# Four embedding squares, one low part and the f = 7 roundings put in other places of their engines' order

## The chip, the cores and the metric

The kernel runs on one core of one Trainium2 chip. The time is device time in microseconds (us); the median of three runs before the change is 703.91 us (702.66 to 705.85). The core has five engines that work side by side: TensorE (PE in the profile) multiplies matrices, VectorE (DVE) and ScalarE (ACT) work elementwise, GpSimd (POOL) does small elementwise work and issues some of the transfers, and SyncE (SP) issues the rest. Each engine takes its instructions in the order of its own queue, so an instruction that has to wait also holds up what stands behind it on the same engine.

## The reference: what is computed

One layer of a decoder block on 512 tokens of width 1024, all in float32:

```python
h = rms_norm(x, g_mix_pre);  z = h @ w_in                 # two token mixers and gates
merged = gate_pool * y_pool + gate_rnn * y_rnn
x = x + rms_norm(merged @ w_o, g_mix_post)
h = rms_norm(x, g_ffn_pre);  up = h @ w_up                # 1024 x 6144
hid = gelu(causal_dwconv(up[:, :3072])) * up[:, 3072:]
x = x + rms_norm(hid @ w_down, g_ffn_post)
ple = rms_norm(p @ w_ple_proj, g_ple_post)                # the embedding
x = x + sigmoid(rms_norm(x, g_ple_gate) @ w_ple_gate) * ple
```

The change touches the passage from the first half to the feed-forward part: the normalised `h` of the second norm (called h2 in the kernel), the statistics of the embedding's norm, and the first pairs of the product with `w_up`.

## The kernel before

**Two parts of each operand.** Products have to be nearly as exact as float32, so each operand is split into a high part (the value rounded to a shorter format) and a low part (the value less its high part). The helper `split` does that in two instructions: ACT copies into the high part (line 195, "rounding" in this document), DVE subtracts (line 191 by way of `sub`). A product is then three matmuls: high by high, high by low, low by high (lines 222 to 224).

**Seven products for eight.** The large products are done in blocks of two by two by a scheme with seven products in place of eight. The seven are called by form numbers f = 1 to 7; forms need sums and differences of blocks, of the activations (made on the chip: `form`, `form_split`) and of the weights. A pair is two column tiles of `w_up` gate and up side; there are twelve, p = 0 to 11. Pair 0 is done plainly (`up_plain`, forms 11, 21, 12, 22), since its products can begin with half of the tokens; pairs 1 to 11 are done in seven products (`up_product`). The order of forms within pair 1 is 1, 6, 2, 5, 7, 4, and from pair 2 on 1, 3 (of the pair before), 6, 2, 7, 5, 4. Weight sums of pairs 1 and 2 are made by transfers in DRAM and loaded, those of later pairs are added by DVE (line 385).

**What follows a product in the up stage.** Forms 1, 6 and 7 accumulate in the same two PSUM banks (`zb`). ACT copies the state out in between: line 1155 after form 1, 1160 after form 6, and after form 7 lines 1162 (into the gate bank `gb`) and 1163 (into the up bank `ub`). Form 4 then accumulates on top of what line 1162 has put into `gb`. The convolution and the gelu of a finished column tile start at line 1168.

**The four h2 tiles.** The normalised tokens come in four tiles of 128. `h2_tile(t)` transposes one by PE (line 1029), in two halves of one PSUM bank each. Each half gives a high part on ACT, a low part on DVE (both to the tiles named C) and two plain copies on ACT (line 1056, to tiles named m), which later make the forms. Tiles are counted 0 to 3 here; the third token tile is tile 2.

**The embedding.** `ple_tile(t)` multiplies a token tile of p with its weight, and copies the two halves out (lines 858 and 859) and to DRAM (line 861). `ple_norm(t)` then takes two squares with row sums on ACT (line 513), adds them on DVE (line 524), takes the reciprocal root on POOL (line 508) and copies the result on DVE into a small tile `rp` (line 867), which is read at the kernel's end.

**Order.** The order on PE is the order of the program. PE goes through tile 2's transposes, pair 0's forms 12 and 22 on the first half of the tokens, tile 3's transposes, form 1 of pair 1 and then pair 0 on the second half:

```python
O_AFTER = (("up", 11), ("up", 21), ("tr", 2), ("up", 12), ("up", 22), ("tr", 3), ("p1", 1))
```

For the other engines a planner puts the instructions in an order at build time, by priority (the order of the program, raised by `tc.high_priority`) and by when it reckons that their inputs are there. `behind(a, b)` adds an edge: a comes after b on the engine, without a wait of its own. Names such as `last_copy`, `last_low`, `h2_done` and `z_done` remember the instructions that such edges point to; `z_done` is the last line 1163 that was traced.

**Weights.** Weights go through a ring of six raw buffers, loaded by SP (line 379 for the up stage), and rings of six high and six low parts. `weight` prepares a key four keys ahead of its use; for the up stage this leads to `up_form(p, f)`. For pair 1's forms 5 and 7 it makes the high part alone (line 416), and `later_low` makes the low part at a place that the main program names. A raw buffer is free for the next load when the low part has been made.

Of the kernel before, what the change touches and what calls it, by code (L numbers as in the profile page):

```python
# [83 lines left out]
def block_kernel(  # L84
# [21 lines left out]
    ACT, V, PE = nc.scalar, nc.vector, nc.tensor  # L106
# [13 lines left out]
    def urgent():  # L120
        return tc.high_priority(offset=URGENT)
# [3 lines left out]
    def nm(s):  # L125
        uid[0] += 1
        return f"{s}{uid[0]}"

    def bank():
        return psum.tile([P, S], F32, tag="ps", name=nm("ps"))  # L130
# [4 lines left out]
    def slot(dt=F32):  # L135
        return mid.tile([P, S], dt, tag="m", name=nm("m"))
# [10 lines left out]
    def parts_of(n):  # L147

        return [wpool.tile([P, D], F32R, tag=t, name=nm(t))[:, :n] for t in ("hi", "lo")]

    def tiny(n=1, dt=F32):
        return small.tile([P, n], dt, tag="s", name=nm("s"))

    def behind(ins, name):
        tc.add_manual_dep(
            ins.ins,
            name,
            mybir.DependencyInfo(mybir.DependencyClass.NoSync, mybir.DependencyReason.DATA),
            reason="order on the engine",
        )  # L160
# [27 lines left out]
    last_copy, last_low, last_sub, h2_done, z_done, paced = [None], [None], [None], [None], [None], [None]  # L188

    def sub(o, a, b):  # L190
        return V.tensor_tensor(o, a, b, ALU.subtract)  # L191

    def split(hi, lo, src):

        last_copy[0] = ACT.copy(hi, src)  # L195
        last_sub[0] = sub(lo, src, hi.bitcast(F32))
        last_low[0] = last_sub[0].ins.name
# [16 lines left out]
    def apart(v):  # L214
        return v.rearrange("p k (b a) -> p k a b", a=2)

    def kept(v):
        return v.rearrange("p k (a b) -> p k a b", a=2)
# [157 lines left out]
    def block(p, f):  # L376

        t = wpool.tile([P, 2, S], F32, tag="raw", name=nm("raw"), bufs=6)
        nc.sync.dma_start(t, usum[p, f] if (p, f) in usum else up_block(p, f))
        return t  # L380
# [3 lines left out]
    def add(o, a, b):  # L384
        V.tensor_tensor(o, a, b, ALU.add)

    def up_form(p, f):

        b = blocks
        if p == 0:  # L390
            t = block(0, f)
        elif p in UP_SUMS:
            t = block(p, {1: 11, 2: 21, 3: 22}.get(f, f))
        elif f == 1:
            for k in (11, 12, 22, 21):
                b[p, k] = block(p, k)
            b[p, 0] = wpool.tile([P, 2, S], F32, tag="sum", name=nm("sum"), bufs=1)
            t = b[p, 11]
        elif f == 6:
            add(b[p, 0], b[p, 11], b[p, 12])  # L400
            t = b[p, 11]
            add(t, b[p, 0], b[p, 22])
        elif f == 7:
            t = b[p, 12]
            add(t, t, b[p, 22])
        elif f == 4:
            t = b[p, 21]
            add(t, b[p, 11], t)
        else:
            t = b[p, {2: 21, 3: 22, 5: 0}[f]]  # L410
        if p == 0 and f != PLAIN[0]:
            late.append((f, t))
            return
        hi, lo = (v.rearrange("p (j c) -> p j c", j=2) for v in parts_of(D))
        if (p, f) in ((1, 5), (1, 7)):
            ins = ACT.copy(hi, t)
            behind(ins, h2_done[0])
            later[f] = hi, lo, t
            ready["up", p, f] = (hi, lo)
            return  # L420
        split(hi, lo, t)
        if p == 1 and f != 1:
            behind(last_copy[0], h2_done[0])
        if (p, f) == (1, 4):
            behind(last_sub[0], hid_done[0])
        if p > 2 and f == 6:
            behind(last_copy[0], z_done[0])
        if p > 1 and f == 3:
            behind(last_copy[0], z6_done[p])
        ready["up", p, f] = (hi, lo)  # L430

    def later_low(f):
        hi, lo, t = later[f]
        last_sub[0] = sub(lo, t, hi.bitcast(F32))
        last_low[0] = last_sub[0].ins.name
# [11 lines left out]
    def prep(key):  # L447
        if key[0] == "up" and key not in parts:
            up_form(*key[1:])
            return  # L450
# [40 lines left out]
    def weight(key, ahead=AHEAD):  # L491
        i = order.index(key)
        while nxt[0] <= min(i + ahead, len(order) - 1):
            prep(order[nxt[0]])
            nxt[0] += 1
        return ready[key]
# [1 line left out]
    def pick(t, a, b):  # L498
        return t[0][:, a:b], t[1][:, a:b]

    last_pow, last_square, last_stat = [None], [None], [None]

    rb = const.tile([P, S], F32, tag="rb", name="rb")

# [6 lines left out]
    def square(v, in_order=True, after=None):  # L511
        s = tiny()
        ins = ACT.activation(rb, v, AF.Square, scale=1.0 / 32.0, accum_out=s)  # L513
        if after is not None:
            behind(ins, after)
        if in_order:
            if last_square[0] is not None:
                behind(ins, last_square[0])
            last_square[0] = ins.ins.name
        return s  # L520

    def rstd_from(sums):
        v = tiny()
        last_stat[0] = V.scalar_tensor_tensor(v, sums[0], EPS, sums[1], ALU.add, ALU.add).ins.name  # L524
        return rsqrt(v)

    def rstd_of(halves, in_order=True, after=None):
        return rstd_from([square(v, in_order, after) for v in halves])
# [40 lines left out]
    for a in range(2):  # L569
        xt = xtok[a]  # L570
        for b in range(2):
            v = xt[:, 2 * b : 2 * b + 2, :]
            t = 2 * a + b
# [7 lines left out]
    for k in range(KD):  # L581
        w = weight(("rx", k // 2), ahead=3)
# [27 lines left out]
    mabs, e, f, s, s2, ncol, n2col = sp  # L610
# [234 lines left out]
    h2f_done, z_copied, hid_done, summed = [None], [None], [None], {}  # L845
# [17 lines left out]

    def ple_norm(t, outs, after):
        s = rstd_of(outs, in_order=False, after=after)
        rp[t] = const.tile([P, 1], F32, tag=f"rp{t}", name=f"rp{t}")
        V.tensor_copy(rp[t], s)

# [70 lines left out]
    for m in range(KD):  # L939
        w = weight(("wpo", m))  # L940
# [85 lines left out]
    def transposed(a):  # L1026
        ps = bank()
        for q in range(4):
            PE.transpose(ps[:, q * P : (q + 1) * P], a[:, q * P : (q + 1) * P], ident)  # L1029
        return ps  # L1030
# [9 lines left out]
            nc.sync.dma_start(xr[t, h], x[t * P : (t + 1) * P, h * S : (h + 1) * S])  # L1040
    h2n, h2f = {}, {}

    def h2_tile(t):
        for h in range(2):
            ps = transposed(h2n[t, h]).rearrange("p (k c) -> p k c", k=4)
            hi, lo = (v[h][t // 2][:, :, t % 2 * P : (t % 2 + 1) * P] for v in (h2h, h2l))
            with tc.high_priority(offset=2 * URGENT if t else URGENT):
                split(kept(hi), kept(lo), apart(ps))
                h2_done[0] = last_copy[0].ins.name
            b, c = divmod(t, 2)  # L1050
            q = 10 * b + h + 11
            if c == 0:
                h2f[q] = {k: slot() for k in (0, 2)}
            for k in (0, 2):
                v = kept(h2f[q][k].rearrange("p (k c) -> p k c", k=2)[:, :, c * P : (c + 1) * P])
                h2f_done[0] = ACT.copy(v, apart(ps[:, k : k + 2, :])).ins.name

# [20 lines left out]
    def x2_sum(t, pair):  # L1080
        with urgent():
            add_norm(pair, g_post, [xr[t, 0], xr[t, 1]])

    def x2_out(t, after=None, stat=None):
        res = [xr[t, 0], xr[t, 1]]
        for h in range(2):
            nc.sync.dma_start(x2d[t * P : (t + 1) * P, h * S : (h + 1) * S], res[h])
        with urgent():
            r = rstd_of(res, after=after)
            for h in range(2):  # L1090
                h2n[t, h] = slot()
                ins = V.scalar_tensor_tensor(h2n[t, h], res[h], r, g_pre[h], ALU.mult, ALU.mult)  # L1092
                if stat is not None:
                    behind(ins, stat)
# [94 lines left out]
    ple_outs = []  # L1189
    for t in range(NT):  # L1190
        with tc.high_priority(offset=3 * URGENT):
            outs = ple_tile(t)
        ple_outs.append(outs)
        if t == 1:
            h2_tile(1)
            late_splits()
            x2_sum(3, (oz[1], o5[:, 1]))
            x2_out(2, h2_done[0], last_stat[0])
        if t == 2:
            x2_out(3, ple_done[0])  # L1200
    for kind, n in O_AFTER:
        if kind == "tr":
            h2_tile(n)
            for t in (n - 2) * 2, (n - 2) * 2 + 1:
                ple_norm(t, ple_outs[t], h2f_done[0])
        elif kind == "up":
            up_plain(n, 0)
        else:
            up_product(n, 1)
# [221 lines left out]
    for h in range(2):  # L1431
        for t in range(NT):
            i = 2 * (t % 2) + h
            o = temp()
            v = ple[t // 2][:, i, :]
            ins = V.scalar_tensor_tensor(v, v, rp[t], gp[:, h, :], ALU.mult, ALU.mult)
# [3 lines left out]
            for a, b in parts:  # L1440
                ps = bank()
                for k in range(KD):
                    if (h, t, k) == (0, 1, 3):
                        x3_tile(2)
                    w = weight(("wpg", k // 2, h), ahead=AHEAD if h or t > 1 else 3 - k // 2)
# [86 lines left out]
```

## Time and profile before

| | |
|---|---|
| median of three runs | 703.91 us |
| the profiled execution: its time | 703.09 us |
| the profiled execution: span from first to last instruction | 701.3 us |
| PE busy | 692.9 us, 99% of the span, 4423 matmuls |
| DVE busy | 591.7 us, 84% |
| ACT busy | 454.4 us, 65% |
| POOL busy | 97.1 us, 14% |
| granted TensorE clock | 1.000 |
| chain that ended last | PE 89%, DVE 4%, DMA 3%, ACT 2% |

The profile is of one execution. In a timeline each row has the start in us from the span's first instruction, the duration, the engine, the line, the operation, the tile written and the tile read, and in brackets the time for which the engine was idle before, with the instruction that ended it. Neighbouring instructions of one kind stand in one row with a count (x4). A list of waits has the engine and line that waited, what it waited for, and three numbers: total us, times, longest. A row of the table by stretch has the stretch, its length, the busy time and the number of instructions of PE, the weight loads, DVE, ACT and POOL, then the granted clock, the transfers' share and GB/s. Matmuls overlap: the next one starts before the last has ended, so PE can be busy all the time and still lose a little.

### The profile page before, as it was taken

What the parts mean: (1) busy time and instruction counts of PE and PEld (TensorE: products, weight loads), DVE (VectorE), ACT (ScalarE), POOL (GpSimd) and SP (SyncE); (2) the same over time, 40 slices, a digit from 0 to 9 for tenths busy, and PEclk for the clock granted to TensorE, in tenths of its full rate; (3) what the DMA queues carried; (4) which work ended last, traced back from release to release, by engine and by line L of the source; (5) the groups of instructions that cost most, each with busy time, mean ns of one, the idle gap of its engine ahead of it and who ended that gap; (6) DMA issues with size and microseconds to landing.
All of it is one profiled execution on the core that took longest, in us unless ns stands there. A gap on an engine that the chain in (4) does not pass through costs nothing.

```text
span 701.3 us, 11599 instructions
## 1 busy us (share of the span) xinstructions
PE 692.9 (99%) x4423; PEld 637.9 (91%) x4423; DVE 591.7 (84%) x772; ACT 454.4 (65%) x693; POOL 97.1 (14%) x123
## 2 busy tenths in 40 slices
PE   8999999999999999999999999999999999999997
PEld 7888888888889998899999999999999888888886
DVE  5698735999849998897999999999999988989962
ACT  5857789934538575487966667766667747665631
POOL 0311231412000000112011211111210210001100
PEclk9999999999999999999999999999999999999999
DMA  8999899999797897865386886896699799968111
GB/s 309 411 306 277 249 249 257 244 275 277 241 347 270 316 368 261 314 226 168 118 320 216 195 267 209 208 265 242 160 218 385 237 300 327 338 215 273 43 61 61
DMA packets 67287, 175.71 MB, mean 251 GB/s; under 512 B 6048, under 2 KB 6688, under 8 KB 66848
## 3 DMA queue, kind: packets, MB, share of 16 engines
q1 hardware_dynamic: 49808, 124.64, 49.3%
q0 software_dynamic: 17280, 50.34, 30.5%
q8 instruction: 35, 0.57, 0.3%
q14 instruction: 20, 0.16, 0.1%
q10 hardware_dynamic: 144, 0.00, 0.0%
HBM read 162.37 MB, written 62.91 MB: 321 GB/s over the span
## 4 chain that ended last, share of the span: by engine, by line
PE 89%; DVE 4%; DMA 3%; ACT 2%; issue 1%; POOL 1%; SPq 0%; DVEq 0%; ACTq 0%
PE ps L222 28%; PE ps L224 28%; PE ps L223 28%; PE ps L587 3%; DVE lo L191 1%; DMA lo<-parts 1%; PE ps L696 1%; ACT rb L513 1%; DMA x2d<-m 1%; DVE m L1092 1%; DMA raw<-in_w_rx_dram 1%; POOL s L508 1%; PE ps L1029 0%; DMA raw<-up2sum 0%; DVE C L191 0%
## 5 line engine op out<-in xcount | busy, mean ns | idle before, releaser
L191 DVE TENSOR_TENSOR lo<-raw,hi 128x1024 fp32r<-128x1024 f32 (+2 forms) x199 | 230.2, 1182 | 46.3 <-ACT hi L477 30.4
L222 PE MATMUL ps<-A,hi 128*128 128x256 f32 (+1 forms) x672 | 211.9, 315 | 0.0
L224 PE MATMUL ps<-A,lo 128*128 128x256 f32 (+1 forms) x672 | 211.5, 315 | 0.0
L223 PE MATMUL ps<-A,hi 128*128 128x256 f32 (+1 forms) x672 | 211.4, 315 | 0.0
L477 ACT CAST hi<-raw 128x1024 fp32r<-128x1024 f32 (+1 forms) x118 | 118.3, 1013 | 60.0 <-PE ps L224 20.0
L222 PEld LDWEIGHTS ps<-A,hi 128*128 128x128 f32 x672 | 128.2, 191 | 8.1 <-issue 1.0
L224 PEld LDWEIGHTS ps<-A,lo 128*128 128x128 f32 x672 | 128.3, 191 | 7.1 <-DVE lo L191 0.2
L223 PEld LDWEIGHTS ps<-A,hi 128*128 128x128 f32 x672 | 128.3, 191 | 6.7
L222 PE MATMUL ps<-C,hi 128*128 128x256 f32 x376 | 103.7, 276 | 1.3 <-ACT ps L1162 0.7
L223 PE MATMUL ps<-C,hi 128*128 128x256 f32 x376 | 103.3, 275 | 0.8 <-DVE C L191 0.8
L224 PE MATMUL ps<-C,lo 128*128 128x256 f32 x376 | 103.2, 274 | 0.0
L195 ACT CAST hi<-raw 128x1024 fp32r<-128x1024 f32 x76 | 78.8, 1054 | 21.2 <-PE ps L223 13.1
L222 PE MATMUL ps<-hi,A 128*128 128x512 f32 x224 | 85.2, 380 | 0.0
L223 PE MATMUL ps<-lo,A 128*128 128x512 f32 x224 | 84.9, 379 | 0.0
L224 PE MATMUL ps<-hi,A 128*128 128x512 f32 x224 | 84.9, 379 | 0.0
L222 PEld LDWEIGHTS ps<-C,hi 128*128 128x128 f32 x376 | 71.8, 191 | 1.9 <-ACT ps L1162 0.9
L223 PEld LDWEIGHTS ps<-C,hi 128*128 128x128 f32 x376 | 71.8, 191 | 1.1 <-DVE C L191 0.9
L224 PEld LDWEIGHTS ps<-C,lo 128*128 128x128 f32 x376 | 71.8, 191 | 0.0
L508 POOL TENSOR_TENSOR s<-s,mhalf 128x1 f32<-128x1 f32 (+1 forms) x21 | 17.4, 828 | 269.0 <-DVE s L524 247.1
L307 POOL DMA_DIRECT2D wdsum<-in_w_down_dram x36 | 33.1, 1056 | 141.5 <-ACT t L1158 62.8
L222 PEld LDWEIGHTS ps<-hi,A 128*128 128x128 f32 x224 | 42.3, 189 | 6.2 <-ACT hi L477 0.3
L224 PEld LDWEIGHTS ps<-hi,A 128*128 128x128 f32 x224 | 42.3, 189 | 6.0
(206 smaller groups left out, 1069.8 us busy)
## 6 DMA issues: line engine op xcount, KB each, us to landing
raw<-in_w_up_dram SPq DMA_DIRECT2D x46, 512.0 KB, 5.9
wdsum<-in_w_down_dram POOLq DMA_DIRECT2D x36, 512.0 KB, 7.5
raw<-in_w_in_dram SPq DMA_DIRECT2D x32, 512.0 KB, 8.4
raw<-wdsum SPq DMA_DIRECT2D x24, 512.0 KB, 8.0
raw<-in_w_down_dram SPq DMA_DIRECT2D x18, 512.0 KB, 6.5
wosum<-in_w_o_dram POOLq DMA_DIRECT2D x12, 512.0 KB, 8.6
wdsum<-wdsum POOLq DMA_DIRECT2D x12, 512.0 KB, 6.0
raw<-wosum SPq DMA_DIRECT2D x8, 512.0 KB, 5.9
```

The costliest lines, as they stand in the source:

```text
L191: return V.tensor_tensor(o, a, b, ALU.subtract)
L195: last_copy[0] = ACT.copy(hi, src)
L222: PE.matmul(o, ah, bh, start=start, stop=False, **kw)
L223: PE.matmul(o, ah, bl, start=False, stop=False, **kw)
L224: PE.matmul(o, al, bh, start=False, stop=stop, **kw)
L307: ins = nc.gpsimd.dma_start(o, i, **kw)
L477: ins = ACT.copy(hi, raw)
L508: last_pow[0] = nc.gpsimd.tensor_tensor(y, v, mhalf[:, :n], ALU.pow).ins.name
L513: ins = ACT.activation(rb, v, AF.Square, scale=1.0 / 32.0, accum_out=s)
L587: PE.matmul(rx[m], a[:, o : o + P], turns(b), start=k == 0 and i == 0, stop=k == KD - 1 and i == 2)
L696: PE.matmul(ps, bd[pr, a, o], turns(b[pr]), start=i == 0, stop=i == 2)
L1092: ins = V.scalar_tensor_tensor(h2n[t, h], res[h], r, g_pre[h], ALU.mult, ALU.mult)
```

## The change

1. In `h2_tile` for tile 2 alone, the four plain copies (line 1056) are no longer traced between the halves but at the end. Ahead of them `ple_norm` is called for embedding tiles 0 and 1. Their four squares stand behind tile 2's last high part, and the four copies behind the last square. Before, the squares stood behind the copies. For tile 3 and embedding tiles 2 and 3 the order stays as it was.
2. The weight of form 1 of pair 1 gets its high part where it did, but its low part is made by `later_low`, behind tile 2's last low part on DVE. Before, it was part of `split`.
3. From pair 2 on the rounding of form 7's weight stands behind `z_done`, the last line 1163 of the pair before. Form 6's had that edge from pair 3 on.

No operation is added or taken away.

```diff
-        if (p, f) in ((1, 5), (1, 7)):
+        if (p, f) in ((1, 1), (1, 5), (1, 7)):
             ins = ACT.copy(hi, t)
-            behind(ins, h2_done[0])
+            if f != 1:
+                behind(ins, h2_done[0])
             later[f] = hi, lo, t
...
         if p > 1 and f == 3:
             behind(last_copy[0], z6_done[p])
+        if p > 1 and f == 7:
+            behind(last_copy[0], z_done[0])
...
     def ple_norm(t, outs, after):
         s = rstd_of(outs, in_order=False, after=after)
+        ple_square[0] = last_any[0]
...
-    def h2_tile(t):
+    def h2_tile(t, then=None):
+        copies = []
...
-                h2f_done[0] = ACT.copy(v, apart(ps[:, k : k + 2, :])).ins.name
+                copies.append((v, apart(ps[:, k : k + 2, :])))
+        after = then() if then else None
+        for v, w in copies:
+            ins = ACT.copy(v, w)
+            if after is not None:
+                behind(ins, after)
+            h2f_done[0] = ins.ins.name
...
+    def early_norms():
+        after = last_copy[0].ins.name
+        for t in (0, 1):
+            ple_norm(t, ple_outs[t], after)
+        return ple_square[0]
+
     for kind, n in O_AFTER:
         if kind == "tr":
-            h2_tile(n)
-            for t in (n - 2) * 2, (n - 2) * 2 + 1:
-                ple_norm(t, ple_outs[t], h2f_done[0])
+            if n == 2:
+                h2_tile(n, early_norms)
+                low = last_low[0]
+                later_low(1)
+                behind(last_sub[0], low)
+            else:
+                h2_tile(n)
+                for t in (2, 3):
+                    ple_norm(t, ple_outs[t], h2f_done[0])
```

`last_any` and `ple_square` remember the name of the last square traced.

More of the change, by code (lines that the diff above doesn't have):

```diff
@@ L499, in pick @@
         return t[0][:, a:b], t[1][:, a:b]
-    last_pow, last_square, last_stat = [None], [None], [None]
+    last_pow, last_square, last_any, last_stat, ple_square = [None], [None], [None], [None], [None]
     rb = const.tile([P, S], F32, tag="rb", name="rb")
@@ L513, in square @@
         ins = ACT.activation(rb, v, AF.Square, scale=1.0 / 32.0, accum_out=s)
+        last_any[0] = ins.ins.name
         if after is not None:
```

## The prediction

> **What bounds the kernel now.** I read TensorE's own waits first, then the busy time by stretch, then TensorE's timeline at each wait, and last the timelines of ScalarE (ACT) and VectorE (DVE) around these places.
>
> ```profile
> PE ps L241 <- DVE mhalf L235: 1.1, 1, 1.1
> PE ps L587 <- ACT hi L474: 0.8, 1, 0.8
> PE ps L223 <- DVE C L191: 0.8, 1, 0.8
> PE ps L222 <- ACT ps L1162: 0.7, 1, 0.7
> PE ps L222 <- ACT C L195: 0.6, 1, 0.6
> ```
> ```profile
> 322.00:352.00 30.00, 27.98 (x244) 27.23 (x243) 26.11 (x42) 28.56 (x56) 4.28 (x4) 1.00 0.32 108
> 360.00:520.00 160.00, 160.00 (x1435) 160.00 (x1435) 150.34 (x163) 107.02 (x173) 27.28 (x33) 1.00 0.80 227
> ```
>
> The first fence is the whole list of TensorE's (PE) idle times. Two are the start. The other three lie close together, and the second shows where: from 322 to 352 PE is busy 27.98 of 30 us, while from 360 to 520 it is never idle, 1435 matmuls in 160 us, 0.11 us each. So PE bounds the kernel, and only what ends these few waits can shorten it. ACT (28.56) and DVE (26.11) are nearly full in that same stretch, so its work comes late by their order, not by PE's.
>
> PE around each wait (start, duration, line, then idle before and releaser):
>
> ```profile
> 324.69 0.28 PE L224 MATMUL ps<-C,lo 128*128 128x256 f32 x1
> 325.53 0.38 PE L222 MATMUL ps<-C,hi 128*128 128x256 f32 x1 [0.57 <-ACT C L195]
> 326.66 0.38 PE L223 MATMUL ps<-C,hi 128*128 128x256 f32 x1 [0.75 <-DVE C L191]
> 326.88 0.27 PE L224 MATMUL ps<-C,lo 128*128 128x256 f32 x1
> ...
> 345.52 0.28 PE L223 MATMUL ps<-A,hi 128*128 128x256 f32 x1
> 345.78 0.38 PE L224 MATMUL ps<-A,lo 128*128 128x256 f32 x1
> ...
> 349.57 0.27 PE L224 MATMUL ps<-C,lo 128*128 128x256 f32 x1
> 350.54 0.38 PE L222 MATMUL ps<-C,hi 128*128 128x256 f32 x1 [0.70 <-ACT ps L1162]
> ```
>
> A matmul's end overlaps the next, so I count starts, less the 0.11 of one. First hold: 0.73 (325.53 after 324.69) and 1.02 (326.66 after 325.53), plus 0.11 for the slow restart (326.88 after 326.66), 1.86 in all. Second: 345.78 after 345.52, 0.15, with a restart taken as the same 0.11: 0.26. It is too short to stand in the waits. Third: 350.54 after 349.57, 0.86, and a restart: 0.97. All that can be won is 1.86 + 0.26 + 0.97 = 3.09 us, 0.44% of the time.
>
> **Squares ahead of the third tile's copies.** ACT:
>
> ```profile
> 315.65 1.10 ACT L195 CAST C<-ps 128x512 fp32r<-128x512 f32 x2
> 320.82 1.24 ACT L1056 COPY m<-ps 128x256 f32<-128x256 f32 x4 [4.06 <-DVE C L191]
> 321.95 0.64 ACT L513 ACTIVATE rb<-m 128x512 f32<-128x512 f32 x1
> ...
> 324.91 1.06 ACT L195 CAST C<-ps 128x512 fp32r<-128x512 f32 x2
> ```
>
> Tile 2's two high parts end at 316.75. The next instruction, the first of four copies (L1056), waits 4.06 us for DVE's low parts of the same PSUM tile. Behind it stand four squares for embedding tiles 0 and 1 (321.95 until 324.91: 2.96 us), and only then tile 3's high parts, for which PE waits at 325.53. Embedding tiles 0 and 1 are in SBUF by then (the embedding copy at 319.50 below is tile 3's), so in front of the copies the squares fit into the idle 4.06 us: 316.7 to 319.6. Their cost there is nothing, and what covers it is that idle time; without it they would cost their 2.96 us again, before the same high parts.
>
> DVE in the same stretch:
>
> ```profile
> 313.96 3.48 DVE L191 TENSOR_TENSOR lo<-raw,hi 128x1024 fp32r<-128x1024 f32 x3
> ...
> 318.17 1.41 DVE L1092 SCALAR_TENSOR_TENSOR m<-m,s,m 128x512 f32<-128x512 f32 x2 [0.66 <-POOL s L508]
> 319.50 0.68 DVE L858 COPY m<-ps 128x512 f32<-128x512 f32 x1
> 320.11 1.28 DVE L191 TENSOR_TENSOR C<-ps,C 128x512 fp32r<-128x512 f32 x2
> 323.47 0.16 DVE L524 SCALAR_TENSOR_TENSOR s<-s,s 128x1 f32<-128x1 f32 x1 [2.09 <-ACT rb L513]
> 324.28 0.15 DVE L867 COPY rp<-s 128x1 f32<-128x1 f32 x1 [0.65 <-POOL s L508]
> ...
> 325.85 0.15 DVE L867 COPY rp<-s 128x1 f32<-128x1 f32 x1 [0.66 <-POOL s L508]
> 325.93 1.28 DVE L191 TENSOR_TENSOR C<-ps,C 128x512 fp32r<-128x512 f32 x2
> ```
>
> The three low parts (3.48, so 1.14 each from start to start) are those of the weights (0,12), (0,22) and (1,1). The last moves behind tile 2's low parts (320.11). What is between, statistic, h2 of tile 3 and an embedding copy, comes forward by 1.14, and tile 2's low parts run from 318.97 to 320.2. The copies then go at about 319.7 and 320.3 and are done near 321.0 instead of 322.06. Were the low parts no earlier, the copies would still end at 322.06 and nothing below would change by more than 0.3 us.
>
> PE, the due times:
>
> ```profile
> 321.25 1.04 PE L1029 MATMUL ps<-ident,m 128*128 128x128 f32 x8
> ...
> 322.34 0.28 PE L224 MATMUL ps<-C,lo 128*128 128x256 f32 x1
> ```
>
> Tile 3's transposes are issued from 321.25 on, and pair 1's first product follows. PE is not late here, so these times stand. Tile 3's first high part can start when the first four of the eight transposes are through, about 321.75, against 324.91: ACT is 3.16 us earlier. Its low part follows on DVE near 322.4, or 323.0 if the two statistics and copies of rp stand in front; before it was 325.93. PE wants them at 324.8 and 324.9. The first hold goes: 1.86 us.
>
> The moved low part is due at PE's third matmul of pair 1, 322.34. Behind tile 2's low parts it runs from 320.2 to 321.35: 1.0 us of slack. Its two neighbours, statistic and rp copies with a root on POOL between, are no longer at 323.47 to 325.9 but somewhere from 319 on; four small instructions of 0.15 us, whose waits cost nothing as long as the low part stands among or before them. ACT's copies also set the banks free that pair 1's first product writes, behind the transposes; ending near 321.0 they are a microsecond ahead of it.
>
> SP's queue is moved too, for the raw buffer that the low part reads is refilled later:
>
> ```profile
> 317.47 0.38 SPq L379 DMA_DIRECT2D raw<-in_w_up_dram  x1
> 320.21 0.80 SPq L861 DMA_DIRECT2D pled<-m  x2
> ```
>
> The load at 317.47, for pair 2's first weight, becomes possible at about 321.4, 3.9 us later; PE reaches that weight only after 350.54, so this is free. If SP's order keeps it ahead of the two embedding stores (320.21), these issue about 1.2 us later. Their buffers are wanted again by the forms on DVE around 325.6; a landing after that takes from DVE's lead, not from PE. I take nothing, with 0 to 1.2 us of lead as the bounds.
>
> **The second hold** is the low part of (1,7), at 344.51 on DVE, the end of a chain through ACT and DVE that starts at tile 3's high parts. The chain moves by 3.16 us and PE by 1.86, a lead of 1.3 us over a lateness of 0.26: the hold goes, 0.26 us. If the stores take 1.2 of the lead, most of it stays.
>
> **Roundings behind copies.** The chain that ended last, around the third hold:
>
> ```profile
> 344.51 1.23 DVE lo L191
> ...
> 345.80 3.27 DMA raw<-up2sum
> ...
> 349.17 1.05 ACT hi L195
> 350.22 0.28 ACT ps L1162
> ```
>
> The low part of (1,7) frees a raw buffer; the load into it (345.80) takes 3.27 us; it is pair 2's block for f = 7, since that pair's sums are loaded in the order 6, 7, 5, 4. Its rounding waits for the load at the head of ACT's queue, and the copy L1162 behind it is what PE waits for at 350.54. With the new edge the rounding stands behind L1163, so the copy goes when PE's product ends. The next product's first twelve matmuls ran until 349.57, so that end was near 348.4; with a copy near 348.7 PE has no hold at 350.54, and 0.97 us goes. The load itself comes some 3 us earlier by the chain above, so even without the edge most of this would. The rounded weight is used four products later, and the delayed rounding costs nothing.
>
> In the later pairs the first of nine alike:
>
> ```profile
> 366.10 0.38 ACT L1163 ACTIVATE ps<-ps 128x256 f32<-128x256 f32 x1
> 366.37 3.08 ACT L195 CAST hi<-raw 128x1024 fp32r<-128x1024 f32 x3
> ```
>
> Here the roundings of f = 6, 2 and 7 already stand behind L1163. The edge changes nothing there.
>
> **Sum.** 1.86 + 0.26 + 0.97 = 3.09, less 0 for the new places: 703.09 - 3.1 = 700.0 us for the profiled execution. The median shown is 703.91, 0.8 above it, so 700.8 is the forecast for a median. Bounds for what replaces a hold: 0 from the rows above, 0.8 to 1.4 from the rival below.
>
> **Where POOL could spoil it.** The roots (L508) on POOL, two of them, and what DVE ran beside the slow one:
>
> ```profile
> 317.60 0.54 POOL L508 TENSOR_TENSOR s<-s,mhalf 128x1 f32<-128x1 f32 x1 [5.60 <-DVE s L524]
> ...
> 330.89 2.66 POOL L508 TENSOR_TENSOR s<-s,mhalf 128x1 f32<-128x1 f32 x1 [5.07 <-DVE s L524]
> ```
> ```profile
> 330.73 1.21 DVE L191 TENSOR_TENSOR lo<-raw,hi 128x1024 fp32r<-128x1024 f32 x1
> ```
>
> The same 128x1 instruction took 0.54 us with DVE waiting and 2.66 us while DVE ran a low part (both inputs in SBUF) and two more such subtractions. With the change two roots come into a stretch where DVE has such work ready. The Trainium skill (SBUF — State Buffer, "Who interferes with whom") says that a VectorE instruction with two SBUF inputs contends with a GpSimd instruction that reads SBUF, and that whoever issues first has the port for the whole instruction; the 2.66 beside 0.54 agrees. By that rule the sum is 3.09 still if only the moved low part runs beside a root, as rp has no reader before the last stage, and it speaks against the change where a DVE copy of rp is queued ahead of what PE needs.
>
> **Rivals.** (1) The low part of (1,1) ends up behind both rp copies. Statistic, root and copy, twice, took 2.46 us (323.47 to 325.93); with the squares long done it is twice 0.81 (323.47 to 324.28), 1.7 with what lies between. The low part would then run from 321.9 at best, 322.6 at worst, until 323.1 or 323.8, and PE would hold at 322.34 for 0.8 to 1.4 us. For: the rp copies come earlier in the program now. Against: the low part is ready when the copies still wait for POOL, so an order by readiness puts it first. Time: 700.8 + 1.1 = 701.9. With one slow root ahead of it (2.66 for 0.54) the hold is 2.1 longer and the time 704.0; that is 0.03 of this rival's chance.
>
> (2) DVE and ACT do not keep the lead. Both are nearly full until 352; if a store or another order costs them 1.3 us or more, the holds at 345.78 and 350.54 stay in part and only the first goes: 703.91 - 1.86 = 702.0. That the change does nothing at all I count here: the squares' edge cannot be without effect, as 4.06 us of idle stand in front of them.
>
> (3) Slower. The order on ACT and DVE is worked out anew over the whole program. If in the nine pairs from 360 on the new edge draws other roundings with it, such that one of them waits at the head of ACT's queue before an L1162, each pair pays what the third hold cost, up to 0.97 us: 703.91 - 3.1 + 8.7 = 709.5. It is slower than before from 0.34 us a pair on. Against it: the roundings of f = 7 already stand where the edge wants them, and four products of 2.7 us (24 matmuls by 0.11) lie between them and their own.
>
> **Chances.** Forecast 0.62, rival 1 0.13, rival 2 0.12, rival 3 0.13. The forecast's own range is 699.5 to 701.7: 3.09 against a median that moves by a microsecond (three runs from 702.66 to 705.85). The overall range, 699.4 to 703.6, takes in rivals 1 and 2. A difference of 0.5% (3.5 us) is about what can be told from none; the holds add up to less, so faster by more needs the median's help: 0.16. Slower by over 0.5% is rival 3: 0.13. Within: 0.71.
>
> **What would show it.** Right: no PE idle between 322 and 352; four squares directly after tile 2's two high parts, with the copies at about 319.7 to 321; tile 3's first high part near 321.8; the copies L1162 of pair 1 with no rounding between them; the later pairs as before. Wrong: a wait of PE on DVE "lo" at 322.3 (rival 1), waits left at about 344 and 348 (rival 2), or idle PE after 360 (rival 3).

## The result, and the profile after

Six runs of the changed kernel had a median of 699.66 us (699.5 to 700.86); six of the kernel before, the three of the time before the change among them, 703.28 us (702.33 to 705.85). The ratio is 0.9944, with a 95% interval from 0.9923 to 0.9966: faster by 0.56%, by at least 0.34 and at most 0.77. A second comparison with more runs, below, gave 0.9960 (0.9944 to 0.9975). The profiled execution took 699.78 us, 3.31 less than the one before.

TensorE's (PE) waits after the change, the whole list, then the busy time by stretch (the columns as before), then the page's shares of the chain that ended last:

```profile
PE ps L241 <- DVE mhalf L235: 1.1, 1, 1.1
```
```profile
322.00:352.00 30.00, 30.00 (x270) 29.95 (x268) 28.76 (x44) 27.82 (x50) 3.77 (x4) 1.00 0.47 149
360.00:520.00 160.00, 160.00 (x1435) 160.00 (x1435) 150.40 (x162) 107.56 (x173) 27.90 (x34) 1.00 0.81 222
```
```profile
PE 99%; DVE 0%; ACT 0%; issue 0%
```

All three waits of the up stage are gone; the one that is left lies in the kernel's first microseconds. PE is busy for the whole of 322 to 352, with 270 matmuls where there were 244, and the rest of the up stage is as it was (1435 matmuls in 160 us). The chain that ended last, 89% on PE before, is now 99% on PE.

The places of the change, first ScalarE (ACT), then VectorE (DVE), then PE (start, duration, line, operation, idle time before). Line numbers have moved: the squares are L516, the plain copies L1065, the transposes L1034.

```profile
315.60 1.10 ACT L195 CAST C<-ps 128x512 fp32r<-128x512 f32 x2
316.56 0.68 ACT L516 ACTIVATE rb<-m 128x512 f32<-128x512 f32 x1
...
319.64 1.24 ACT L1065 COPY m<-ps 128x256 f32<-128x256 f32 x4
321.84 1.08 ACT L195 CAST C<-ps 128x512 fp32r<-128x512 f32 x2 [0.95 <-PE ps L1034]
```
```profile
318.93 1.27 DVE L191 TENSOR_TENSOR C<-ps,C 128x512 fp32r<-128x512 f32 x2
320.12 1.21 DVE L191 TENSOR_TENSOR lo<-raw,hi 128x1024 fp32r<-128x1024 f32 x1
...
323.01 1.28 DVE L191 TENSOR_TENSOR C<-ps,C 128x512 fp32r<-128x512 f32 x2
```
```profile
321.20 1.04 PE L1034 MATMUL ps<-ident,m 128*128 128x128 f32 x8
...
322.30 0.28 PE L224 MATMUL ps<-C,lo 128*128 128x256 f32 x1
...
324.75 0.28 PE L222 MATMUL ps<-C,hi 128*128 128x256 f32 x1
324.87 0.27 PE L223 MATMUL ps<-C,hi 128*128 128x256 f32 x1
...
343.63 0.28 PE L223 MATMUL ps<-A,hi 128*128 128x256 f32 x1
343.74 0.28 PE L224 MATMUL ps<-A,lo 128*128 128x256 f32 x1
```

The squares start at 316.56, directly behind tile 2's high parts, and fill the time until the copies can go at 319.64. Tile 3's high parts start at 321.84, as soon as the transposes of 321.20 let them, and before it was 324.91. Tile 2's low parts are at 318.93, the moved low part directly behind at 320.12 until 321.3, a microsecond before PE's third matmul of pair 1 (322.30). Where PE had stood for 1.86 us, it goes from 324.75 to 324.87 in step. The second hold, too short for the list of waits, is gone as well: its two matmuls (345.52 and 345.78 before) are at 343.63 and 343.74, one pitch of 0.11 apart.

The third place, ACT around the copies after form 7 of pair 1 (now L1174 and L1175):

```profile
346.39 0.36 ACT L1174 COPY ps<-ps 128x256 f32<-128x256 f32 x1 [0.69 <-PE ps L224]
...
346.94 1.07 ACT L195 CAST hi<-raw 128x1024 fp32r<-128x1024 f32 x1
```

The copy now waits for PE alone, and the rounding of pair 2 stands behind it.

### The profile page after: what moved, and what is told of

It reads as the page before. It is cut to its first block, busy times and chain, and to the rows that moved or that the text cites. A ratio compares the mean times of both kernels' runs of the same rounds, so it can differ in the third digit from the quotient of the medians.

```text
span 698.0 us, 11598 instructions
## 1 busy us (share of the span) xinstructions
PE 692.4 (99%) x4423; PEld 638.1 (91%) x4423; DVE 591.4 (85%) x772; ACT 453.9 (65%) x693; POOL 97.1 (14%) x123
## 4 chain that ended last, share of the span: by engine, by line
PE 99%; DVE 0%; ACT 0%; issue 0%
PE ps L222 31%; PE ps L223 31%; PE ps L224 31%; PE ps L591 3%; PE ps L1034 1%; PE ps L700 1%; PE ps L241 1%; PE ps L642 0%; ACT t L166 0%; DVE t L1474 0%; DVE t L1475 0%; PE ps L1160 0%; DVE m L233 0%; DVE mhalf L235 0%
## 5 line engine op out<-in xcount | busy, mean ns | idle before, releaser
L224 PEld LDWEIGHTS ps<-hi,A 128*128 128x128 f32 x224 | 42.3, 189 | 6.0
L223 PEld LDWEIGHTS ps<-lo,A 128*128 128x128 f32 x224 | 42.4, 189 | 5.9
```

The source lines that it names most:

```text
L223: PE.matmul(o, ah, bl, start=False, stop=False, **kw)
L224: PE.matmul(o, al, bh, start=False, stop=stop, **kw)
```

## The experiments

All kernels below compute the same as the kernel before. Since one difference of 1 us is 0.14%, the times alone tell little; the traces tell more. Two rows of each are enough. One is the start of tile 3's transposes, which in all traces comes before the first hold. The other is the span. What lies between them is the up stage and all that follows. For the kernel before it is 701.3 - 321.25 = 380.05 us, for the kernel after 698.0 - 321.20 = 376.8.

| kernel | tile 3's transposes | span | from there on | median us (runs) | ratio to before, 95% |
|---|---|---|---|---|---|
| before, profiled first | 321.25 | 701.3 | 380.05 | | |
| before again | 320.68 | 700.5 | 379.8 | 702.80 (12) | 0.9996 (0.9987 to 1.0006) |
| part 1: squares | 321.43 | 698.5 | 377.1 | 700.32 (11) | 0.9962 (0.9950 to 0.9974) |
| part 2: low part | 321.48 | 700.2 | 378.7 | 701.74 (12) | 0.9975 (0.9964 to 0.9985) |
| part 3: rounding | 320.68 | 699.6 | 378.9 | 701.82 (12) | 0.9981 (0.9971 to 0.9991) |
| parts 1 and 2 | 322.08 | 699.3 | 377.2 | 700.03 (6) | 0.9952 (0.9935 to 0.9970) |
| parts 1 and 3 | 321.30 | 698.1 | 376.8 | 699.94 (5) | 0.9950 (0.9930 to 0.9970) |
| parts 2 and 3 | 321.48 | 699.3 | 377.8 | 700.91 (6) | 0.9971 (0.9959 to 0.9982) |
| whole change, profiled first | 321.20 | 698.0 | 376.8 | 699.66 (6) | 0.9944 (0.9923 to 0.9966) |
| whole change again | 321.51 | 698.3 | 376.8 | 700.38 (12) | 0.9960 (0.9944 to 0.9975) |
| low part last | 321.48 | 699.2 | 377.7 | 701.08 (12) | 0.9970 (0.9958 to 0.9983) |
| root beside low part | 321.91 | 698.7 | 376.8 | 700.31 (10) | 0.9965 (0.9950 to 0.9979) |
| mixer edge | 321.26 | 698.0 | 376.7 | 700.70 (7) | 0.9963 (0.9949 to 0.9977) |

The experiments were run in three sets, each on another chip and beside its own runs of the kernel before. Only the first set (before again and parts 1, 2 and 3) has a trace of the kernel before; its 379.8 stands for all.

**The kernel before, again.** No edit.

> The kernel before, unchanged, against itself. Theory A (the 0.56% is the holds of PE, 3.1 us, and what was measured beyond it is the spread of the executions of before, 702.33 to 705.85): ratio 1.000 with an interval that is as wide as 0.002 to each side, some executions near 702.4 and some near 705, and a trace with the same three holds of 1.86, 0.26 and 0.97 us. Rival B (the slower executions have longer holds, since the third one depends on a transfer): where the profiled execution is slower than 703.1, its holds add up to more than 3.1 us.

Its waits (PE's list):

```profile
PE ps L241 <- DVE mhalf L235: 1.1, 1, 1.1
PE ps L223 <- DVE C L191: 0.8, 1, 0.8
PE ps L222 <- ACT ps L1162: 0.7, 1, 0.7
PE ps L222 <- ACT C L195: 0.5, 1, 0.5
```

The ratio of the same kernel to itself is 0.9996, and 34 runs taken beside it have a median of 703.03 us, between 701.99 and 706.24. The three holds are there again and as long (0.8, 0.7 and 0.5 in the list), so theory A holds. Rival B is about slower executions, and this one, at 702.27 us, is not slower than 703.1; it is not tested here. But the span is 0.8 us shorter, and 0.57 of it was there before the holds: the transposes are at 320.68 and not at 321.25. The wait for the first high part of the input (L587 on L474, 0.8 us in the first profile) is missing from this list. So the profiled executions of one kernel differ in the first microseconds. What PE waits for there is not the same from trace to trace; the list of parts 1 and 2 shows the largest:

```profile
PE ps L589 <- ACT A L559: 1.6, 1, 1.6
...
```

1.6 us of wait at the start (L589, the first product), and the transposes at 322.08. In the table the column behind the transposes has no such spread: the three traces without a hold in the up stage (whole change, whole change again, parts 1 and 3) agree within 0.05.

**Squares alone.** The text of the change, without the new case for form 1 of pair 1, `later_low(1)` and the edge for form 7:

```diff
             if n == 2:
                 h2_tile(n, early_norms)
-                low = last_low[0]
-                later_low(1)
-                behind(last_sub[0], low)
```

> Squares ahead of tile 2's copies alone. Theory A: the first hold goes (1.86), the second goes (0.26), since tile 3's high parts start near 322.1 where they started at 324.9, and the third shrinks from 0.97 to about 0.3, since the load of pair 2's block comes some 2.8 us earlier: about 2.8 us less than before. Rival C (the three parts are each worth their own hold): only the first hold goes, 1.9 us less, and 0.97 is left at L1162.

SP's issue of the load for pair 2's form 7, ACT behind it, and PE:

```profile
343.11 2.06 SPq L379 DMA_DIRECT2D raw<-up2sum  x2
```
```profile
346.51 1.05 ACT L195 CAST hi<-raw 128x1024 fp32r<-128x1024 f32 x1 [0.58 <-PE ps L223]
347.46 0.37 ACT L1171 COPY ps<-ps 128x256 f32<-128x256 f32 x1
```
```profile
347.65 0.27 PE L224 MATMUL ps<-C,lo 128*128 128x256 f32 x1
347.89 0.38 PE L222 MATMUL ps<-C,hi 128*128 128x256 f32 x1
```

379.8 - 377.1 = 2.7 us, and 2.7 in the medians (703.03 - 700.32). The first and the second hold are gone, and the third has shrunk without its edge, since the load goes out at 343.11 and not at 345.80: 347.89 after 347.65 is 0.13 beyond the 0.11 of one matmul, with the slow restart 0.24 in all. Theory A had 0.3; rival C's 0.97 is out. One part takes nearly everything.

**Low part alone.**

```diff
-        if (p, f) in ((1, 5), (1, 7)):
+        if (p, f) in ((1, 1), (1, 5), (1, 7)):
...
             h2_tile(n)
+            if n == 2:
+                low = last_low[0]
+                later_low(1)
+                behind(last_sub[0], low)
```

> The low part of pair 1's first weight behind tile 2's low parts, alone. Theory A: copies and squares come 1.14 us earlier, tile 3's high parts start near 323.8 where they started at 324.9, and the first hold shrinks from 1.86 to 0.6 to 0.8; the rest as before: 1.0 to 1.3 us less. Rival C (this part only makes room and is worth nothing alone): no difference, the first hold stays at 1.86.

```profile
325.03 0.28 PE L222 MATMUL ps<-C,hi 128*128 128x256 f32 x1
325.72 0.38 PE L223 MATMUL ps<-C,hi 128*128 128x256 f32 x1 [0.42 <-DVE C L191]
```

PE (above) holds for 325.72 - 325.03 - 0.11 = 0.58 and a restart of 0.1, where it was 1.86; the wait for the high part is gone, the one for DVE's low part is left. 379.8 - 378.7 = 1.1 us, 1.3 in the medians. So this part is worth something alone: it brings the copies and with them the squares forward, to 319.87 and 321.00 from 320.82 and 321.95.

**Rounding alone.**

```diff
             behind(last_copy[0], z6_done[p])
+        if p > 1 and f == 7:
+            behind(last_copy[0], z_done[0])
```

> The edge for the roundings of form 7 alone. Theory A: only pair 2's rounding changes its place, the third hold (0.97) goes, the other two stay: 1.0 us less. Rival D (the later pairs matter, too): more than 1.5 us less, or PE loses time after 360.

PE's waits, then ACT:

```profile
PE ps L241 <- DVE mhalf L235: 1.1, 1, 1.1
PE ps L223 <- DVE C L191: 0.8, 1, 0.8
PE ps L222 <- ACT C L195: 0.5, 1, 0.5
```
```profile
347.95 0.36 ACT L1164 COPY ps<-ps 128x256 f32<-128x256 f32 x1
...
348.52 1.05 ACT L195 CAST hi<-raw 128x1024 fp32r<-128x1024 f32 x1
```

The wait on ACT's copy is gone, the other two are there, and 379.8 - 378.9 = 0.9 us (1.2 in the medians). The order of instructions on all engines differs from that before in this one place: the rounding of pair 2 changes places with two copies. In pairs 3 to 11 nothing moved, as the prediction had read from the rows at 366; nothing of rival D is seen.

**Pairs of parts.** Without the edge (parts 1 and 2):

```diff
-        if p > 1 and f == 7:
-            behind(last_copy[0], z_done[0])
```

> Without the edge for the roundings. Theory A: pair 2's rounding stands ahead of L1162 again, but its load now comes near 346.1, so the copy is late by 0 to 0.2 us only: 2.9 to 3.1 us less than before, the same as the whole change within what can be told. Rival C (each part its own hold): 2.1 us less, and 0.97 at L1162.

Without the move of the low part (parts 1 and 3), the edit of the squares alone with the edge kept:

> Without the move of the low part. Theory A: the squares alone free ACT for tile 3's high parts, so the first hold stays away, and the edge takes the rest of the third: 3.1 us less, the same as the whole change. Rival C (the move has a share of its own): 1 us less gain than the whole change, as it had alone.

Without the squares (parts 2 and 3), both edits shown above in one kernel:

> Low part and edge without the squares. Theory A: as the low part alone did, the first hold shrinks to 0.6 to 0.7, the second stays at 0.25, the third goes with the edge: 2.1 us less than before. Rival C (each part its own hold): 1.0 us less, from the edge.

ACT and PE of parts 1 and 2, and of PE's waits of parts 2 and 3 the one in the up stage:

```profile
347.36 1.08 ACT L195 CAST hi<-raw 128x1024 fp32r<-128x1024 f32 x1 [0.78 <-DMA raw<-up2sum]
```
```profile
348.30 0.27 PE L224 MATMUL ps<-C,lo 128*128 128x256 f32 x1
348.76 0.38 PE L222 MATMUL ps<-C,hi 128*128 128x256 f32 x1 [0.19 <-ACT ps L1172]
```
```profile
PE ps L223 <- DVE C L191: 0.5, 1, 0.5
```

Parts 1 and 3 give the same 376.8 as the whole change: beside the squares the moved low part adds nothing that the trace shows. Without the edge PE still holds 348.76 - 348.30 - 0.11 = 0.35 and a restart, because the rounding waits 0.78 us for its load; I had expected 0 to 0.2. In this execution the rounding started 3.58 us after the load's issue (343.78), in part 1's 3.40 (343.11). So the two traces say no more than that the hold without the edge is a few tenths and depends on when the load lands. Parts 2 and 3 leave the rest of the first hold and the second: 379.8 - 377.8 = 2.0 us, as expected. Alone the three parts gave 2.7, 1.1 and 0.9, 4.7 together; the whole change gives 3.0. They overlap, because the first two end the same hold and an earlier chain ends most of the third.

**The whole change again.** No edit to the changed kernel.

> The whole change again, beside many executions of before. Theory A (the gain is the holds of PE, 3.1 us): ratio 0.9956, 3.0 to 3.3 us less, so just under 0.5%. Rival B (there is a gain beyond the holds): 3.6 us or more less, as in the first comparison (0.9944).

The ratio is 0.9960, 2.85 us between the medians (703.23 over 24 runs, 700.38 over 12). From the transposes on it is 376.8 as in the first trace, 3.0 less than the kernel before in its second trace. The distances from one start to the next on PE say the same. Behind 318 us no start in this trace, or in the first one of the change, comes more than 0.06 us later after its predecessor than the median over all thirteen traces has it; in the second trace of before seven starts do, all at the three holds, and they add up to 3.0 us. That speaks for theory A. The first comparison's 0.9944 is not contradicted: its interval holds 0.9960.

**The low part last.** The moved low part behind the second copy of rp (`rp_done` is that copy's name):

```diff
-                low = last_low[0]
+                low = rp_done[0]
                 later_low(1)
                 behind(last_sub[0], low)
```

> The whole change, but with the moved low part behind both copies of rp (rival 1 of the prediction made true). Theory A: the copies of rp are done near 322.0, the low part ends near 323.1, PE holds for 0.8 to 1.1 us at its third matmul of pair 1 (322.3) and nothing else changes: 0.8 to 1.1 us slower than the whole change. Rival E (PE's hold is taken out of later slack, or the roots are slowed by DVE's work to 2.66 us): 0.3 us or less, or 2 us and more.

DVE, then PE:

```profile
321.21 0.15 DVE L874 COPY rp<-s 128x1 f32<-128x1 f32 x1 [0.65 <-POOL s L511]
...
322.08 0.15 DVE L874 COPY rp<-s 128x1 f32<-128x1 f32 x1 [0.66 <-POOL s L511]
322.16 1.22 DVE L191 TENSOR_TENSOR lo<-raw,hi 128x1024 fp32r<-128x1024 f32 x1
```
```profile
322.46 0.28 PE L223 MATMUL ps<-C,hi 128*128 128x256 f32 x1
323.43 0.38 PE L224 MATMUL ps<-C,lo 128*128 128x256 f32 x1 [0.69 <-DVE lo L191]
323.64 0.28 PE L222 MATMUL ps<-C,hi 128*128 128x256 f32 x1
```

The two copies of rp each wait 0.65 us for POOL, the low part starts at 322.16, and PE holds at its third matmul for 323.43 - 322.46 - 0.11 = 0.86 and a restart of 0.1: 0.96. From the transposes on it is 377.7 against 376.8. What the prediction set down for its first rival, 0.8 to 1.4, is what this place costs; the change did not run into it, since the order put the low part first.

**A root beside the low part.** One more edge puts the moved low part behind tile 0's statistic as well, so that the root and the low part start together:

```diff
                 behind(last_sub[0], low)
+                behind(last_sub[0], stat_of[0])
```

> The whole change with tile 0's statistic ahead of the moved low part, so that its root runs on POOL while DVE makes the low part (both inputs in SBUF). Theory F (such work holds the root): the root takes 1.3 to 1.6 us in place of 0.54 and ends some 0.4 us after the low part, and PE, whose low part is there by 321.5, loses nothing. Rival G (the slow root of 2.66 us had another cause): 0.54 us.

DVE, then POOL:

```profile
320.79 0.15 DVE L528 SCALAR_TENSOR_TENSOR s<-s,s 128x1 f32<-128x1 f32 x1
320.85 1.22 DVE L191 TENSOR_TENSOR lo<-raw,hi 128x1024 fp32r<-128x1024 f32 x1
```
```profile
321.02 1.46 POOL L511 TENSOR_TENSOR s<-s,mhalf 128x1 f32<-128x1 f32 x1 [3.39 <-DVE s L528]
322.81 0.54 POOL L511 TENSOR_TENSOR s<-s,mhalf 128x1 f32<-128x1 f32 x1 [0.34 <-DVE s L528]
```

The root beside the low part took 1.46 us, until 322.48, 0.4 after the low part's end at 322.07; the next one, with DVE waiting, took 0.54. The Trainium skill (SBUF — State Buffer, "Who interferes with whom") has a VectorE instruction with two SBUF inputs contend with a GpSimd instruction that reads SBUF; the 1.46 beside 0.54 agrees with it. PE lost nothing: 376.8. Tile 3's low parts do stand behind both copies of rp, but they start at 323.46, and PE reaches the matmul that needs the first of them at 325.58. Before the change that matmul went 0.73 us after the low parts had started (326.66 and 325.93), so some 1.4 us are to spare.

**One more edge of this kind, in the mixer stage.** PE has a hold of 0.22 us at 241, where the rounding of a weight (pair 1, form 3 of the recurrent mixer's output product) stands ahead of a copy that PE needs:

```diff
+            if key == ("rg", 1, 3):
+                behind(ins, z_copied[0])
```

> The whole change, and the same kind of edge for one rounding in the mixer stage, the weight of pair 1, form 3, behind the copies after form 7 of pair 0, where PE still has a hold of 0.22 us at 241. Theory A: that hold goes and nothing else, 0.2 us less than the whole change, too little to be told in the times. Rival H (the order is worked out anew, and roundings and squares far from the edge change places with it): PE shows holds in other places, and the time is 0.5 us or more longer.

PE at the hold, in the whole change and then with the edge, and at a new place, with the low part on DVE that it waits for there:

```profile
240.80 0.28 PE L224 MATMUL ps<-C,lo 128*128 128x256 f32 x1
241.03 0.38 PE L222 MATMUL ps<-C,hi 128*128 128x256 f32 x1
```
```profile
240.08 0.28 PE L224 MATMUL ps<-C,lo 128*128 128x256 f32 x1
240.19 0.28 PE L222 MATMUL ps<-C,hi 128*128 128x256 f32 x1
...
271.98 0.48 PE L224 MATMUL ps<-hi,A 128*128 128x512 f32 x1 [0.74 <-DVE A L191]
```
```profile
270.71 1.22 DVE L191 TENSOR_TENSOR A<-C,A 128x1024 fp32r<-128x1024 f32 x1
```

The hold at 241 is gone: 0.11 between the two starts, where the whole change has 0.23. A new one, on a low part of DVE, stands at 272, 0.74 us of idle time. This one edge gave ACT, DVE and SP another order in several places, some of them 50 and 70 us later. The column from the transposes on begins behind both places and says nothing of them; from the matmul before the old hold to tile 3's transposes it is 81.18 us here and 80.40 in each of the twelve other traces, so the edge won 0.2 us and lost 1.0. PE came to 272 earlier than in any other trace, but that alone does not explain the hold: in the twelve others this low part starts 1.55 to 1.80 us before its matmul is due, also where PE is early, and here 0.4. So the new order is the likely cause, in one trace. Rival H came true in the trace, but not in the times: 0.9963 cannot be told from the whole change, and 0.8 us is too little for them. The version is no better. No kernel here is told apart from the whole change as faster; parts 1 and 3 are as fast by the trace.

## Why the prediction was right and where it was wrong

**The three holds.** "1.86 + 0.26 + 0.97 = 3.09 us": right. All three went, and the traces give 3.0 us (379.8 to 376.8) or 3.25 against the first trace of before. Most of the 0.25 between those two is a short hold of the first trace that the prediction did not list: it looked at 322 to 352 and at the list of waits, and a hold of 0.18 us at 605 stood in neither. The second trace of before and those of the changed kernel do not have it. PE's rows of the kernel before there:

```profile
604.24 0.38 PE L223 MATMUL ps<-lo,A 128*128 128x512 f32 x1
604.46 0.38 PE L224 MATMUL ps<-hi,A 128*128 128x512 f32 x1
604.79 0.46 PE L222 MATMUL ps<-hi,A 128*128 128x512 f32 x1
605.08 0.38 PE L223 MATMUL ps<-lo,A 128*128 128x512 f32 x1
```

604.24 to 604.46 is one matmul of this size, 0.22; the next two starts are 0.33 and 0.29 later, 0.18 more than the pitch together.

**The times on the engines.** Squares 316.7 to 319.6: measured 316.56 to 319.6. Copies from 319.7, done near 321.0: 319.64 to 320.88. Tile 3's first high part near 321.75: 321.84. Its low part at 322.4, or 323.0 if the copies of rp stand in front: 323.01. The moved low part from 320.2 to 321.35: 320.12 to 321.33. They are right because the change gave the engines no other order than the one written down, which the order of instructions on all engines confirms: four squares, one low part, one rounding, and SP's load behind the two embedding stores, not ahead of them. The stores thus went earlier, and the prediction's bound of 1.2 us for them was not needed.

**The roundings.** Right that only pair 2's moves and that most of the third hold goes without the edge: 0.24 was left with the squares alone, 0.46 with parts 1 and 2.

**The shares.** Right, too, that without the moved low part nothing would change by more than 0.3 us: parts 1 and 3 give 376.8 like the whole change. What the prediction did not say is what each part takes alone. The shares are not a sum: the squares alone take 2.7, the low part 1.1 alone, and beside the squares nothing that can be seen.

**The rivals.** The first is real where it is made to happen (0.96 us); the change avoided it. Neither of the other two occurred.

**Where it was wrong.** The forecast was 700.8 us and "within 0.5%" with 0.71; measured were 699.66 us and 0.56%. Two steps failed. The first is "the median shown is 703.91, 0.8 above it, so 700.8 is the forecast for a median". The 0.8 was carried over from three runs, and it was not a property of the kernel: 34 runs of the kernel before had a median of 703.03 and 24 others 703.23. In the changed kernel the median lies 0.12 below the profiled execution in the first comparison (699.66 and 699.78) and 0.29 above it in the second (700.38 and 700.09). Of the 1.14 us between 700.8 and 699.66 this term is 0.92, and the other 0.22 is what the profiled execution gained beyond the sum (3.31 for 3.09). The sum against the profiled execution itself, 700.0, was a little nearer to both measured medians of the changed kernel than the 700.8.

The second is "the holds add up to less, so faster by more needs the median's help: 0.16". The gain by the traces is 0.43% (3.0 of 703), so close to the bound of 0.5% that the scatter decided on which side a set of six runs fell: the first comparison put it above, the second, with 24 and 12 runs, at 0.40%. The 3.62 us of the first comparison are 3.09 of the sum, 0.22 more in the profiled execution (0.18 of it the hold at 605) and 0.31 from where the medians lie beside the profiled executions (0.19 above before, 0.12 below after); nothing in the traces makes that a part of the gain.

The mechanism and its size stand; the chance of 0.16 was too small for a sum that lies 0.4 us from the bound, with medians that move by more than that. Neither 0.40 nor 0.56% is settled by its own interval. The four comparisons of kernels whose traces have no hold behind 318 us and the same order up to there (the whole change twice, parts 1 and 3, the root beside the low part) gave 0.56, 0.40, 0.50 and 0.35%, 0.45% in the mean, close to the 0.43% of the traces.

## What to carry to other kernels

Where the bounding engine is busy nearly all the time, the holds are found by the starts of its instructions, and what can be won is their sum; here that sum was right to within 0.2 us. An instruction that waits at the head of an in-order queue holds up what does not need to wait, so independent work belongs in front of it: four squares of 3 us went into an idle time of 4 us, and that one move gave 2.7 of the 3.0 us. Parts of a change that end the same hold do not add up, and a forecast near the bound of what can be measured should be split over both sides of it.

## What the runs showed that was not expected

The profiled executions of one and the same program differ mostly in their first microseconds; slower ones, up to 707 us, were not profiled. The place of tile 3's transposes, 320.68 to 322.08 over all traces, takes in that scatter (1.4 us); behind it two traces of the changed kernel agree within 0.1 us. A difference of 1 us between two kernels is better read from a fixed instruction to the end of the trace than from the times.
